# Row maxima on one core: loads of three rows in two places for two rows in three, and a table of places for the last 28 rows

## The chip, the core and the metric

The kernel runs on one core of one Trainium2 chip. The engines that matter: the sixteen DMA engines of the core, which bring data from HBM into the on-chip memory (SBUF, 128 partitions); SyncE (SP), which issues loads and the last store; ScalarE (ACT), which issues the other store; and VectorE (DVE), which reduces. GpSimd (POOL) only clears semaphores at the end, and TensorE has no work.

The metric is the time of one execution on the device, in microseconds (us), as the median of several runs.

## The reference

```
def reference(x):                      # x: 8192 x 8192, float32, normal
    return np.linalg.norm(x, ord=np.inf, axis=1)
```

The infinity norm of each row: the largest absolute value among its 8192 elements. 268.44 MB go in, 32 KB come out.

## The kernel before

Each of the 128 partitions holds 64 whole rows of `x` in the course of the run, 8192 elements (32 KB) each. VectorE's `reduce_max` with absolute values (L253) takes a stretch of a partition's data and leaves one number, or one per row when it gets several whole rows in one instruction. All data pass through one tile, `ring` (49664 elements per partition), and all results collect in `r_bulk` and `r_tail`.

**The bulk (L261 to L269).** 40 rows per partition come in 20 loads of `B` = 2 rows (16384 elements per partition, 8.4 MB). They go to `SLOTS` = 3 places of the ring in turn. Each load is followed by one reduction of two rows into `r_bulk`. A place is used again when its reduction is done, so two loads can be under way or queued while a third is being reduced.

**The end (`TAIL`, L20 to L31, and L272 to L317).** The last 24 rows per partition lie side by side as 196608 elements and come in 37 loads, listed in `TAIL` as (start in the data, width), the widths falling from 16384 to 512. A load need not hold whole rows: L272 to L280 cut each load into pieces at the row borders. A piece that isn't the last of its row is reduced to one number, which is written into the ring just ahead of the place where the row's last piece will land (`slot`); the row's last piece is then reduced together with those numbers into `r_tail`. The places are worked out in order around the ring (L283 to L294), each aligned to `PAD` = 128.

**Order.** SP issues all loads in the program's order. A load waits for the reductions that read the part of the ring that it overwrites (a semaphore that VectorE counts up), and, as there are eight semaphores for transfers, for the landing of the load eight before it. VectorE takes the reductions in program order and waits for each load's semaphore. `r_bulk` is stored from ACT after the reductions of the third last load (L314 to L317), `r_tail` from SP after the last one (L318).

Four functions that run over the finished program (L319 to L322) are the same in both kernels: they drop waits that another wait implies, move the first load ahead of the program's opening, let POOL do the ending, and leave VectorE out of the opening.

Of the kernel before, what the change touches and what calls it, by code (L numbers as in the profile page):

```python
# [16 lines left out]

HEAD, STEP = 32, 8

TAIL = [  # L20
    (0, 16384), (16384, 16384), (32768, 16384), (49152, 15488),
    (64640, 14336), (78976, 12800), (91776, 11392), (103168, 10112),
    (113280, 9088), (122368, 8064), (130432, 7296), (137728, 6528),
    (144256, 5760), (150016, 5248), (155264, 4608), (159872, 4096),
    (163968, 3712), (167680, 3328), (171008, 2944), (173952, 2688),
    (176640, 2432), (179072, 2176), (188416, 1920), (181248, 1792),
    (190336, 1536), (183040, 1408), (191872, 1280), (184448, 1152),
    (193152, 1024), (185600, 896), (194176, 768), (186496, 768),
    (194944, 640), (187264, 640), (195584, 512), (187904, 512),
    (196096, 512),  # L30
]  # L31


# [177 lines left out]
@with_exitstack  # L211
def kernel(
    ctx: ExitStack,
    tc: tile.TileContext,
    x: bass.AP,
    out: bass.AP,
    G: int = 4,
    B: int = 2,
    SLOTS: int = 3,
    PAD: int = 128,  # L220
):
    nc = tc.nc
    P = nc.NUM_PARTITIONS
    rows, cols = x.shape
    W = B * cols
    R = SLOTS * W + PAD * 4


    n_tail = sum(w for _, w in TAIL) // cols
    met = 0  # L230
    for lo, w in sorted(TAIL):
        assert lo == met
        met += w
    assert met == n_tail * cols
    n_bulk_rows = rows // P - n_tail
    assert n_bulk_rows % (G * B) == 0
    A = n_bulk_rows // (G * B)
    split = n_bulk_rows * P
    x_b = x[:split].rearrange("(a p n b) c -> a n p (b c)", p=P, a=A, n=G, b=B)
    out_b = out[:split].rearrange("(a p n b) -> p a (n b)", p=P, a=A, n=G, b=B)  # L240
    x_t = x[split:].rearrange("(p t) c -> p (t c)", p=P)
    out_t = out[split:].rearrange("(p t) -> p t", p=P)

    pool = ctx.enter_context(tc.tile_pool(name="sbuf", bufs=1))
    r_bulk = pool.tile([P, A, G * B], F32)
    r_tail = pool.tile([P, n_tail], F32)
    used = [HEAD, A * G * B, n_tail]
    gap = -sum(-(-n // STEP) * STEP for n in used) % PAD
    pool.tile([P, gap], F32, name="gap")
    ring = pool.tile([P, R], F32)  # L250

    def absmax(o, i):
        return nc.vector.reduce_max(  # L253
            out=o, in_=i, axis=X, apply_absolute_value=True
        )

    def after(ins, first, kind):
        info = mybir.DependencyInfo(kind, mybir.DependencyReason.SCHED_ONLY)
        tc.add_manual_dep(ins.ins, first.ins.name, info, reason="order")

    for a in range(A):  # L261
        for n in range(G):
            at = (a * G + n) % SLOTS * W
            t = ring[:, at : at + W]
            nc.sync.dma_start(out=t, in_=x_b[a, n])
            absmax(
                r_bulk[:, a, n * B : (n + 1) * B],
                t.rearrange("p (b c) -> p b c", b=B),
            )  # L269


    pieces = []  # L272
    for j, (at, w) in enumerate(TAIL):
        end = at + w
        while at < end:
            r = at // cols
            to = min(end, (r + 1) * cols)
            pieces.append((j, r, to - at))
            at = to
    of_row = [[k for k, s in enumerate(pieces) if s[1] == r] for r in range(n_tail)]  # L280


    here = A * G % SLOTS * W  # L283
    start, slot = [], []
    for j, (_, w) in enumerate(TAIL):
        first = next(s for s in pieces if s[0] == j)
        ks = of_row[first[1]]
        n_part = len(ks) - 1 if pieces[ks[-1]][0] == j else 0
        at = -(-(here + n_part) // PAD) * PAD
        if at + w > R:  # L290
            at = -(-n_part // PAD) * PAD
        start.append(at)
        slot.append(at - n_part)
        here = at + w  # L294

    for j, (src, w) in enumerate(TAIL):
        at = start[j]
        nc.sync.dma_start(out=ring[:, at : at + w], in_=x_t[:, src : src + w])
        here = [k for k, s in enumerate(pieces) if s[0] == j]
        offs = [at + sum(pieces[i][2] for i in here[:m]) for m in range(len(here))]  # L300
        todo = list(zip(here, offs))
        if slot[j] != at:

            todo = todo[1:] + todo[:1]
        for k, lo in todo:
            _, r, n = pieces[k]
            ks = of_row[r]
            if k == ks[-1]:
                frm = slot[j] if len(ks) > 1 else lo
                done = absmax(r_tail[:, r : r + 1], ring[:, frm : lo + n])  # L310
            else:
                to = slot[pieces[ks[-1]][0]] + ks.index(k)
                done = absmax(ring[:, to : to + 1], ring[:, lo : lo + n])
        if j == len(TAIL) - 3:  # L314

            ins = nc.scalar.dma_start(out=out_b, in_=r_bulk[:])
            after(ins, done, mybir.DependencyClass.Sync)  # L317
    nc.sync.dma_start(out=out_t, in_=r_tail[:])  # L318
    nc.at_finalize(drop_implied_waits)  # L319
    nc.at_finalize(start_first_load_early)  # L320
    nc.at_finalize(finish_on_pool)
    nc.at_finalize(open_without_vector)  # L322
# [30 lines left out]
```

## Time and profile before

| what | value |
|---|---|
| time, median of 3 runs | 626.67 us (626.62 to 627.07) |
| the profiled execution's own time | 626.65 us |
| its span, first to last instruction | 624.0 us |
| VectorE busy | 553.1 us, 76 instructions |
| 20 reductions of two rows | 344.4 us, 17220 ns each |
| loads | 57, 268.44 MB, 430 GB/s over the span |
| VectorE's waits for loads | 62.1 us before the bulk's reductions, 7.9 us later |

How to read it: "busy" is the time in which an engine executes; for the DMA queues it is the time that their packets took, as a share of sixteen engines' span. A packet is what one DMA engine moves for one descriptor. In the timeline the columns are start, duration, engine, line, operation, what it writes and reads with partitions x elements, how many were merged, and the idle time before them with what ended it. In the chain of waits they are start, duration, and what the chain went through. In the waits they are the engine and line, what it waited for, the total in us, how many times, and the longest. In the groups of instructions, the busy time in us, the mean duration in ns, and the idle time before them. "SPq" and "ACTq" are the queues from which SP and ACT issue transfers. The packed trace also has a record of each DMA packet (start, duration, size) and of each count that a transfer's engines add to its semaphore; sixteen such counts make a landing.

### The profile page before, as it was taken

Reading aid. Unit: us, or ns where it says so; the run is one execution under the profiler, and the core shown is the slowest. Engines: PE = TensorE matmul, PEld = TensorE weight load, DVE = VectorE, ACT = ScalarE, POOL = GpSimd, SP = SyncE. Lnnn points to the kernel's source line nnn. Section 1 sums busy time; section 2 is a strip of 40 time slices with the busy share of each in tenths; the row PEclk is TensorE's granted clock in tenths of the full one; section 3 lists DMA queues with packets and bytes.
Section 4 is the critical chain, followed back from the end, with each engine's and each line's share of the span. In section 5 each row is a group of like instructions: output and inputs, shape, how many; then the busy total and the mean of one; then the engine's idle time right before and its main releaser. Section 6 shows DMA issues by size and latency. Waiting matters only on the chain.

```text
span 624.0 us, 166 instructions
## 1 busy us (share of the span) xinstructions
DVE 553.1 (89%) x76; POOL 0.2 (0%) x4
## 2 busy tenths in 40 slices
DVE  0588988889988899888898888988899999999999
POOL 0000000000000000000000000000000000000000
DMA  9999999999999999999999999999999999999998
GB/s 403 454 420 454 420 441 433 408 466 403 471 403 454 420 454 420 450 424 429 445 408 466 403 466 408 454 420 454 409 435 445 422 436 428 429 427 431 429 425 343
DMA packets 8865, 268.47 MB, mean 430 GB/s; under 512 B 1568, under 2 KB 1568, under 8 KB 3488
## 3 DMA queue, kind: packets, MB, share of 16 engines
q1 hardware_dynamic: 8208, 268.44, 99.7%
q10 hardware_dynamic: 656, 0.02, 0.1%
q14 instruction: 1, 0.01, 0.0%
HBM read 268.44 MB, written 0.03 MB: 430 GB/s over the span
## 4 chain that ended last, share of the span: by engine, by line
DMA 61%; DVE 38%; issue 0%; DVEq 0%
DMA ring<-in_x_dram 61%; DVE r_bulk L253 19%; DVE ring L253 10%; DVE r_tail L253 9%; DVEq L348 0%
## 5 line engine op out<-in xcount | busy, mean ns | idle before, releaser
L253 DVE TENSOR_REDUCE r_bulk<-ring 128x2 f32<-128x16384 f32 x20 | 344.4, 17220 | 62.1 <-DMA ring<-in_x_dram 62.1
L253 DVE TENSOR_REDUCE r_tail<-ring 128x1 f32<-128x8192 f32 (+14 forms) x24 | 109.7, 4587 | 7.7 <-DMA ring<-in_x_dram 7.7
L253 DVE TENSOR_REDUCE ring<-ring 128x1 f32<-128x5248 f32 (+26 forms) x32 | 101.5, 3215 | 0.2 <-DMA ring<-in_x_dram 0.2
L337 POOL MEMSET const-bfloat16-1.0<- 128x1 bf16 x1 | 0.1, 101 | 0.0
L337 POOL MEMSET const-uint8-127<- 128x1 uint8 x1 | 0.1, 101 | 0.0
L337 POOL MEMSET const-float32-0.0<- 128x1 f32 x1 | 0.1, 98 | 0.2 <-issue 0.2
L337 POOL MEMSET const-float32-1.0<- 128x1 f32 x1 | 0.1, 98 | 0.0
## 6 DMA issues: line engine op xcount, KB each, us to landing
ring<-in_x_dram SPq DMA_DIRECT2D x1, 7744.0 KB, 39.6
ring<-in_x_dram SPq DMA_DIRECT2D x1, 7168.0 KB, 37.2
ring<-in_x_dram SPq DMA_DIRECT2D x1, 6400.0 KB, 33.0
ring<-in_x_dram SPq DMA_DIRECT2D x1, 5696.0 KB, 36.7
ring<-in_x_dram SPq DMA_DIRECT2D x1, 5056.0 KB, 41.0
ring<-in_x_dram SPq DMA_DIRECT2D x1, 4544.0 KB, 36.0
ring<-in_x_dram SPq DMA_DIRECT2D x1, 4032.0 KB, 31.9
ring<-in_x_dram SPq DMA_DIRECT2D x1, 3648.0 KB, 40.2
```

The source lines that it names most:

```text
L253: return nc.vector.reduce_max(out=o, in_=i, axis=X, apply_absolute_value=True)
L337: nc = _bacc.Bacc("TRN2", target_bir_lowering=False, num_devices=1)
```

## The change

Four edits, all in the tile kernel and its table:

- The bulk's loads are three rows wide (`B` = 3, 24576 elements per partition, 12.6 MB) and use two places (`SLOTS` = 2). There are 12 of them, for 36 rows.
- The end has 28 rows in 35 loads. `TAIL` now lists (place in the ring, start in the data, width); the places are no longer worked out. The widths fall from 24576 to 768. The ring has a fixed size, `R` = 52992.
- Where a load of the end holds several whole rows in a run, one reduction takes them together. With the wider loads of the bulk, VectorE has 50 reductions instead of 76.
- Each load is ordered behind the one before it (no semaphore), and a load whose row has numbers waiting ahead of its place is ordered behind the reduction that wrote them.

In the built program a load wider than 16384 elements per partition has two descriptors for each partition instead of one (128 x 2 x 12288 for a load of 24576).

```diff
 TAIL = [
-    (0, 16384), (16384, 16384), (32768, 16384), (49152, 15488),
-    (64640, 14336), (78976, 12800), (91776, 11392), (103168, 10112),
...
-    (194944, 640), (187264, 640), (195584, 512), (187904, 512),
-    (196096, 512),
+    (0, 0, 24576), (24576, 24576, 23552), (0, 49152, 20864),
+    (20864, 73728, 16384), (0, 90112, 16384), (37248, 106496, 11392),
+    (16384, 122880, 8192), (24576, 131072, 8192), (0, 139264, 8192),
+    (8192, 147456, 8192), (32768, 155648, 8192), (16384, 163840, 8192),
+    (24576, 172032, 7424), (0, 180224, 7040), (7040, 188416, 6016),
...
+    (51968, 48128, 1024), (38016, 228352, 1024), (43904, 203904, 896),
+    (50944, 72832, 896), (48512, 179456, 768),
 ]
...
-    B: int = 2,
-    SLOTS: int = 3,
+    B: int = 3,
+    SLOTS: int = 2,
+    R: int = 52992,
     PAD: int = 128,
...
-    R = SLOTS * W + PAD * 4
...
-    for a in range(A):
-        for n in range(G):
-            at = (a * G + n) % SLOTS * W
-            t = ring[:, at : at + W]
-            nc.sync.dma_start(out=t, in_=x_b[a, n])
-            absmax(
-                r_bulk[:, a, n * B : (n + 1) * B],
-                t.rearrange("p (b c) -> p b c", b=B),
-            )
+    loads = []
+
+    def load(lo, n, src):
+        ins = nc.sync.dma_start(out=ring[:, lo : lo + n], in_=src)
+        if loads:
+            after(ins, loads[-1], mybir.DependencyClass.NoSync)
+        loads.append(ins)
+
+    for k in range(A * G):
+        at = k % SLOTS * W
+        load(at, W, x_b[k // G, k % G])
+        absmax(
+            r_bulk[:, k // G, k % G * B : (k % G + 1) * B],
+            ring[:, at : at + W].rearrange("p (b c) -> p b c", b=B),
+        )
...
             r = at // cols
-            to = min(end, (r + 1) * cols)
-            pieces.append((j, r, to - at))
-            at = to
+            n = min(end, (r + 1) * cols) - at
+            if n == cols:
+                n = (end - at) // cols * cols
+            pieces.append((j, r, n))
+            at += n
...
+    part = {}
+    for j, (at, src, w) in enumerate(TAIL):
+        load(at, w, x_t[:, src : src + w])
+        if slot[j] != at:
+            after(loads[-1], part[slot[j]], mybir.DependencyClass.Sync)
...
-            if k == ks[-1]:
-                frm = slot[j] if len(ks) > 1 else lo
-                done = absmax(r_tail[:, r : r + 1], ring[:, frm : lo + n])
-            else:
+            if k != ks[-1]:
                 to = slot[pieces[ks[-1]][0]] + ks.index(k)
                 done = absmax(ring[:, to : to + 1], ring[:, lo : lo + n])
+                part[slot[pieces[ks[-1]][0]]] = done
+            elif len(ks) > 1:
+                done = absmax(r_tail[:, r : r + 1], ring[:, slot[j] : lo + n])
+            else:
+                b = n // cols
+                t = ring[:, lo : lo + n].rearrange("p (b c) -> p b c", b=b)
+                done = absmax(r_tail[:, r : r + b], t)
```

## The prediction, made before the changed kernel had run

> **What bounds the kernel now.** I read the page first: the busy lines and the queues.
>
> ```profile
> span 624.0 us, 166 instructions
> ## 1 busy us (share of the span) xinstructions
> DVE 553.1 (89%) x76; POOL 0.2 (0%) x4
> ...
> q1 hardware_dynamic: 8208, 268.44, 99.7%
> ...
> q14 instruction: 1, 0.01, 0.0%
> ```
>
> The load queue q1 keeps its sixteen DMA engines busy for 99.7% of the span; VectorE (DVE) is busy for 89%. The bytes are fixed, so a gain must come from the first 2 us, the last 2 us, or small costs between packets. The waits say who is early and who is late, then the timeline gives the rhythm.
>
> ```profile
> DVE r_bulk L253 <- DMA ring<-in_x_dram: 62.1, 20, 22.1
> ```
>
> ```profile
> 22.11 17.22 DVE L253 TENSOR_REDUCE r_bulk<-ring 128x2 f32<-128x16384 f32 x1 [22.11 <-DMA ring<-in_x_dram]
> 41.40 17.22 DVE L253 TENSOR_REDUCE r_bulk<-ring 128x2 f32<-128x16384 f32 x1 [2.08 <-DMA ring<-in_x_dram]
> 60.74 17.22 DVE L253 TENSOR_REDUCE r_bulk<-ring 128x2 f32<-128x16384 f32 x1 [2.12 <-DMA ring<-in_x_dram]
> ...
> 572.92 10.08 DVE L253 TENSOR_REDUCE ring<-ring 128x1 f32<-128x5248 f32 x2 [0.24 <-DMA ring<-in_x_dram]
> ...
> 621.95 1.28 DVE L253 TENSOR_REDUCE r_tail<-ring 128x1 f32<-128x519 f32 x2
> 622.07 0.41 ACTq L316 DMA_DIRECT2D out_dram<-r_bulk  x1
> 623.26 0.35 SPq L318 DMA_DIRECT2D out_dram<-r_tail  x1
> ```
>
> VectorE waits about 2.1 us for every load of two rows. The landings behind those starts, 22.08 to 447.19 us over 22 intervals, are 19.32 us apart. The chain of waits shows how early a load is issued:
>
> ```profile
> 39.34 0.02 issue
> 39.35 40.76 DMA ring<-in_x_dram
> 80.11 0.02 issue
> ```
>
> A load issued at 39.35 lands at 80.11, behind the load that lands at 60.72: SP issues 21.4 us before the queue would run dry. So DMA is the bound with a large reserve, and the end is the last landing (622.41 in the trace) plus 0.82 us of VectorE (to 623.23) plus 0.77 us to the end of the span.
>
> **The change part by part.** Sums are against the profiled span, 624.0; that execution took 626.65, and the median is 626.67, so I add 2.67 to a span.
>
> *Descriptors and loads.* In the packet records each load is cut into one packet per partition and one 4-byte semaphore packet per engine: 57 x 144 = 8208, the page's count. A packet of 65536 B starts 2.416 us after the one before it on its engine, one of 2048 B 0.080 us: 36.8 ps per byte plus 0.0047 us per packet; the semaphore packet adds 0.006. The built program turns every load wider than 16384 into two packets per partition: 15 such loads, 47 in all. An engine then handles 15 x 16 + 32 x 8 = 496 data packets for 456, so 40 x 0.0047 = +0.19, and ten semaphores fewer, 10 x 0.006 = -0.06. Bounds: -0.44 if a load costs 0.044 whatever its packets (8 x 0.0047 + 0.006), +0.19 if the semaphores are free.
>
> *The instruction fetch.* The one q14 packet after the start comes at 570.05 and takes 0.31 us on one DMA engine. Until then the first and last engine of a load finish 0.85 to 0.98 us apart; at the landing of 572.89 it is 1.29, and that landing comes 0.34 us later than its bytes ask (6.56 us against 5248/16384 x 19.32 + 0.03 = 6.22). VectorE's 0.24 us wait at 572.92 shows it: the fetch fell on the slowest engine. It comes 0.85 us after VectorE began its 48th reduction, with no other engine's instruction near. The new program has 50 reductions and reaches the 48th after the loads have been read, so I take -0.33; 0 if the fetch is another engine's or comes earlier.
>
> The Trainium skill ("Runtime: NRT & Kernel Launch", section "Instruction fetch mechanics") says that instruction memory is refilled in blocks of 256 instructions, mostly hidden. The trace differs: 8 KB, with 76 VectorE instructions, and not hidden. By the page no instruction count here would need a fetch, this term would be 0 and the time 627.0.
>
> *The end.* The rows:
>
> ```profile
> L253 DVE TENSOR_REDUCE ring<-ring 128x1 f32<-128x768 f32 x2 | 1.8, 942 | 0.0
> ...
> L253 DVE TENSOR_REDUCE r_tail<-ring 128x1 f32<-128x519 f32 x2 | 1.3, 683 | 0.0
> ```
>
> The last load is 768 wide instead of 512. It lands 768/16384 x 19.28 + 0.044 = 0.95 us after the one of 896, whose reduction holds VectorE 0.99 us (1.075 less 0.083 that neighbours overlap). So the last one starts some 0.07 us after landing and takes 0.943: 1.01 to 1.04 instead of 0.82, +0.20. The two stores wait for the same things as before. 26 VectorE instructions fewer save 26 x 0.06 us (a back-to-back step is 1.0417 ns per element plus 0.06) = 1.6 us, worth nothing: VectorE waits for landings at both ends.
>
> *Two places instead of three.* This removes the reserve. Per load of three rows the transfer is 1.5 x 19.32 + 0.04 = 29.0 us; the reduction 17.22 plus one more row (17.22 - 8.69 = 8.53) = 25.75, and 0.05 for two semaphores. SP can issue load k only when load k-2 is reduced: 29.0 - 25.8 = 3.2 us before load k-1 lands, not 21.4. This holds at twelve handoffs: loads 3 to 12 of the bulk and the table's first two. Two others are tighter. The table's third load (20864 at place 0) waits for the reduction of the first while the second, only 23552 wide (27.8 us), flies: 27.8 - 25.8 = 2.0. Its fifth (16384 at place 0) waits for two rows of the third, 17.2 + 0.1, against 19.3 for the fourth: 2.0 again. All others have 7 us or more. SP has nothing else queued behind these waits than later loads, whose places come free later still.
>
> What a handoff costs depends on the time from SP's issue until a DMA engine runs at full rate. The slowest engine ends its last packet 0.34 us before a landing, so it has 2.9 us at the twelve and 1.7 at the two; the fastest has 0.9 less, but it may also idle 0.9 without moving the end. The trace shows no load that comes to a nearly empty queue in mid-stream. Lower end: the final stores, issued at 622.07 and 623.26, have their first packets 0.96 and 0.84 us later. Upper end: the very first load, issued at 0.00, has first packets at 0.99 to 2.22, and by its landings (21.17 to 22.08, less 0.32 and 8 x 2.416) reaches full rate 1.5 to 2.4 us after issue. I take 1.0: at a handoff the queue is running and the reads of the last packets cover the start, as in the stores; the first load also had to start sixteen idle engines (its first packets took 2.5 to 3.2 us, later ones 2.42). At 1.0 the slowest engine never empties; a fast one idles 0.2 us, or some 0.8 with a fresh start, inside its 0.9. Cost 0; by the upper end 2 x (2.4 - 1.7) = 1.4 to 1.5.
>
> **Sum:** 624.0 + 0.19 - 0.06 - 0.33 + 0.20 + 0 = 624.0, so 626.7: no change. Own range 626.2 to 627.3.
>
> **The rivals.**
>
> *A: the two tight handoffs run dry.* For it: the nearest HBM load, the first, needed 2.4 us on its slowest engine, over the 1.7 at hand. Against it: half of that is a cold start. Price from 1.0 at 2.2 us to 1.5 at 2.4: 627.7 to 628.2. It decides from 1.7 us on.
>
> The Trainium skill ("DMA: Bandwidth & Descriptors", section "Latency and other measured facts") puts the first byte of a hardware queue at about 0.6 us and an HBM access under high load at 2 us. No run here shows either in mid-stream. Together 2.6 us, an estimate: 0.9 at each tight handoff and 628.5.
>
> *B: every handoff runs dry.* One mechanism, slower than before: under a saturated HBM a fresh load needs over 2.9 us. The twelve handoffs pay the excess each, the two tight ones 1.2 more each. At 3.2: 12 x 0.3 less what the engines' spread absorbs, some 2 to 4 us, and 2 x 1.5 = 5 to 7: about 632. Against it: no row above 2.4.
>
> *C: loads are priced per load, not per packet.* -0.44 instead of +0.13: 626.1. Against it: the two-point fit above.
>
> **How the numbers follow.** Forecast 0.42, A 0.28, B 0.20, C 0.06, something faster that I don't see 0.04. Changes under 0.2% (1.25 us; about what a measurement of this kernel can tell from no change) are 625.4 to 627.9. Same: the forecast, C, and 0.10 of A below 627.9: 0.58. Slower: 0.18 of A and B: 0.38. Faster: 0.04, since the whole start and end offer hardly 1.2 us. The range reaches from C's 626.1, less 0.2, over all of A and the start of B: 625.9 to 630.0, leaving out some 0.18.
>
> **What would show it.** Handoffs right: VectorE waits 3.2 us before each bulk reduction but the first, landings 29.0 us apart, and 27.8 and 24.6 for the table's second and third load. A shows as 25.3 instead of 24.6 (third load) and 20.0 instead of 19.3 (fifth); B as bulk intervals above 29.1 and a q1 share below 99.5%. The fetch term is right if no q14 packet comes before 620 us. The end is right if the last reduction ends 1.0 us after the last landing. The prediction is wrong if any handoff opens a gap on the slowest engine.

## The result, and the profile after

| | before | after |
|---|---|---|
| time, median of 6 runs each | 626.72 us (626.62 to 627.13) | 637.91 us (637.30 to 639.51) |
| ratio, 95% interval | | 1.0181 (1.0168 to 1.0195) |
| span of the profiled execution | 624.0 us | 635.2 us |
| last landing | 622.41 us | 633.44 us |

The change costs 11.2 us, 1.8%. The forecast was no change, and the time lies outside the range. The page of the changed kernel, span, busy lines and queues:

```profile
span 635.2 us, 126 instructions
...
DVE 551.0 (87%) x50; POOL 0.2 (0%) x4
...
q1 hardware_dynamic: 8688, 268.44, 99.0%
q10 hardware_dynamic: 400, 0.02, 0.0%
```

VectorE does as much as before. The load queue's share falls from 99.7% to 99.0%: the DMA engines now have gaps. Gaps are the smaller part of the loss: 99.0% of 635.2 is 628.8 us of packet time per engine, against 622.1 before, so packets also take some 6.7 us longer in all. There is no q14 line any more. The waits put most of VectorE's idle time before the bulk, as before, but with the wait before the first load 31.8 instead of 22.1 us:

```profile
DVE r_bulk L256 <- DMA ring<-in_x_dram: 74.2, 12, 31.8
```

The timeline of the changed kernel, VectorE's reductions in the bulk and at the start of the table:

```profile
31.79 25.75 DVE L256 TENSOR_REDUCE r_bulk<-ring 128x3 f32<-128x24576 f32 x1 [31.79 <-DMA ring<-in_x_dram]
60.79 25.75 DVE L256 TENSOR_REDUCE r_bulk<-ring 128x3 f32<-128x24576 f32 x1 [3.24 <-DMA ring<-in_x_dram]
90.11 25.75 DVE L256 TENSOR_REDUCE r_bulk<-ring 128x3 f32<-128x24576 f32 x1 [3.57 <-DMA ring<-in_x_dram]
...
178.32 25.75 DVE L256 TENSOR_REDUCE r_bulk<-ring 128x3 f32<-128x24576 f32 x1 [3.29 <-DMA ring<-in_x_dram]
208.82 25.75 DVE L256 TENSOR_REDUCE r_bulk<-ring 128x3 f32<-128x24576 f32 x1 [4.75 <-DMA ring<-in_x_dram]
...
388.44 25.75 DVE L256 TENSOR_REDUCE r_tail<-ring 128x3 f32<-128x24576 f32 x1 [5.18 <-DMA ring<-in_x_dram]
416.33 17.22 DVE L256 TENSOR_REDUCE r_tail<-ring 128x2 f32<-128x16384 f32 x1 [2.13 <-DMA ring<-in_x_dram]
```

A wait of 3.2 us means that the load came on the 29.0 us beat. Waits of 4.8 and 5.2 mean that it landed 1.5 and 2.0 us late: 178.32 to 208.82 is 30.5 us. Thirteen loads on a beat of 28.98 us (1.5 times the 19.32 of before) would have the last one in at 31.77 + 12 x 28.98 = 379.5; it lands at 388.42, so 8.9 us go here. By the 29.00 us that lead_7 (below) keeps it is 8.6. The chain of waits of the changed kernel (start, duration, what it went through) shows the new limit:

```profile
57.57 32.51 DMA ring<-in_x_dram
90.08 0.02 issue
90.11 25.77 DVE r_bulk L256
...
175.05 33.75 DMA ring<-in_x_dram
208.80 0.02 issue
208.82 25.77 DVE r_bulk L256
...
354.06 34.36 DMA ring<-in_x_dram
...
414.22 27.34 DMA ring<-in_x_dram
...
458.83 23.18 DMA ring<-in_x_dram
```

Load and reduction alternate: a load is issued when a reduction has freed its place, and the next reduction waits for that load. The load issued at 175.05 takes 33.75 us, although its bytes need 29.0 and the load ahead of it lands after 3.24. From here on, the *lead* is the time from a load's issue to the landing of the load ahead, and the *loss* is what its landing is late against the beat.

Of the 11.03 us by which the last landing moved, the eleven handoffs up to 388.42 hold 8.9, the table's second load 0.1, its third (issued at 414.22, lands 25.26 us after the one ahead, its bytes ask 24.64) 0.6, and its fifth (issued at 458.83, 21.10 for 19.32) 1.8. With +0.13 for packets and -0.33 for the fetch as predicted that is 11.2, 0.2 more than measured: the price of the bulk's added packets (29.00 instead of 28.98 us per load) is in the 8.9 already and is counted twice.

### The profile page after: what moved, and what is told of

It is laid out like the page before. It is cut to its first block, busy times and chain, and to the rows that moved or that the text cites. A ratio compares the mean times of both kernels' runs of the same rounds, so it can differ in the third digit from the quotient of the medians.

```text
span 635.2 us, 126 instructions
## 1 busy us (share of the span) xinstructions
DVE 551.0 (87%) x50; POOL 0.2 (0%) x4
## 4 chain that ended last, share of the span: by engine, by line
DMA 50%; DVE 50%; DVEq 0%; issue 0%
DMA ring<-in_x_dram 50%; DVE r_bulk L256 24%; DVE r_tail L256 17%; DVE ring L256 8%; DVEq L361 0%
## 5 line engine op out<-in xcount | busy, mean ns | idle before, releaser
L256 DVE TENSOR_REDUCE r_bulk<-ring 128x3 f32<-128x24576 f32 x12 | 309.0, 25753 | 74.2 <-DMA ring<-in_x_dram 74.2
L256 DVE TENSOR_REDUCE r_tail<-ring 128x1 f32<-128x8192 f32 (+11 forms) x22 | 170.2, 7783 | 9.2 <-DMA ring<-in_x_dram 9.2
L256 DVE TENSOR_REDUCE ring<-ring 128x1 f32<-128x7168 f32 (+15 forms) x16 | 72.6, 4578 | 0.1
```

What stands on the lines that cost most here:

```text
L256: return nc.vector.reduce_max(out=o, in_=i, axis=X, apply_absolute_value=True)
```

## The experiments

Medians are set against the kernel before, run on the same chip (626.6 to 626.7 in each batch).

| kernel | leads in the bulk, us | loss in the bulk, us | time, us | ratio, 95% interval |
|---|---|---|---|---|
| after | 3.2 to 5.1 | 8.9 | 637.91 | 1.0181 (1.0168 to 1.0195) |
| one_row_loads | 3.1 to 6.5 | 9.5 | 639.32 | 1.0194 (1.0177 to 1.0211) |
| lead_3_7 | 3.7 to 5.1 | 6.2 | 636.11 | 1.0157 (1.0137 to 1.0177) |
| lead_4 | 4.2 to 4.4 | 0.55 | 630.60 | 1.0061 (1.0048 to 1.0075) |
| lead_5 | 5.2 | 0.25 | 630.29 | 1.0057 (1.0041 to 1.0072) |
| lead_7 | 7.3 | 0.28 | 630.64 | 1.0059 (1.0044 to 1.0075) |
| half_bulk_reduce | 16.0 | 0.44 | 630.29 | 1.0059 (1.0044 to 1.0074) |
| released_by_parts | 21 and 32 | 0.52 | 628.53 | 1.0030 (1.0019 to 1.0041) |
| all_leads_long | 21 and 32 | 0.55 | 627.28 | 1.0011 (1.0002 to 1.0019) |
| before_two_places | 2.0 to 6.0 | 22.5 | 650.31 | 1.0375 (1.0359 to 1.0390) |
| two_places_lead_4 | 4.2 to 4.5 | 0.26 | 626.92 | 1.0005 (0.9996 to 1.0014) |
| before_two_descriptors | 21 | 0.7 | 627.62 | 1.0016 (1.0007 to 1.0026) |
| two_queues | no load ahead | | 671.76 | 1.0718 (1.0701 to 1.0734) |

Leads and losses are those of the one profiled execution. The loss is against 28.98 us per load, 19.32 us for loads of two rows. In the kernels whose leads are all 5 us or more, what is listed is not loss at handoffs but mostly the price of added packets, 0.02 to 0.04 us per load; released_by_parts and all_leads_long also have one landing each that is about 0.25 us late with a lead of 21 us.

**half_bulk_reduce: the same loads, a long lead.** From the changed kernel:

```diff
-            ring[:, at : at + W].rearrange("p (b c) -> p b c", b=B),
+            ring[:, at : at + W].rearrange("p (b c) -> p b c", b=B)[:, :, : cols // 2],
```

> The changed kernel, but each bulk reduction reads only the first half of each of its three rows (the other half of 36 rows per partition is left out of the result). Loads, places and descriptors are those of the changed kernel; a reduction takes about 12.9 us instead of 25.75, so a bulk load is issued about 16 us before the one ahead of it lands, instead of 3.2. Theory 1 (too little lead: a load issued 3 us ahead reaches the DMA engines too late): the 8.9 us that the bulk lost vanish, the table's third and fifth load still lose about 2.4; 629 us. Theory 2 (the 272 descriptors of a load take too long to be written, but only when the lead is short): the same, 629. Theory 3 (loads of two descriptors per partition, or the new row pitch, are slower by themselves): still about 638.

Its timeline, the bulk's second and third reduction:

```profile
60.60 12.95 DVE L256 TENSOR_REDUCE r_bulk<-ring 128x3 f32<-128x12288 f32 x1 [16.06 <-DMA ring<-in_x_dram]
89.60 12.95 DVE L256 TENSOR_REDUCE r_bulk<-ring 128x3 f32<-128x12288 f32 x1 [16.05 <-DMA ring<-in_x_dram]
```

Every wait is 16 us and the beat is 29.0. Loads, descriptors and places are those of the changed kernel, so nothing in the loads alone makes the loss; Theory 3 falls. The table's two tight handoffs, which the edit leaves alone, still lose 3.9 us (25.52 for the third load, 22.31 for the fifth), which is the 3.9 us of the span above before's.

**one_row_loads: no wide descriptors, the same lead.** From the changed kernel, each bulk load as three:

```diff
-        load(at, W, x_b[k // G, k % G])
+        for i in range(B):
+            load(at + i * cols, cols, x_b[k // G, k % G, :, i * cols : (i + 1) * cols])
```

> The changed kernel, but each bulk load is issued as three loads of one row with one descriptor per partition, all three still released by the one reduction of three rows. The lead of the first of them stays 3.2 us. Theory 1 (lead alone): 637 to 638, as the changed kernel. Theory 2 (the late engines are late because a load's 272 descriptors are written one after another): the first load's 144 descriptors arrive in half the time, most of the bulk's 8.9 us vanish; 629 to 631.

Its timeline, the bulk's second to fourth reduction:

```profile
60.56 25.75 DVE L256 TENSOR_REDUCE r_bulk<-ring 128x3 f32<-128x24576 f32 x1 [3.27 <-DMA ring<-in_x_dram]
90.79 25.75 DVE L256 TENSOR_REDUCE r_bulk<-ring 128x3 f32<-128x24576 f32 x1 [4.47 <-DMA ring<-in_x_dram]
119.94 25.75 DVE L256 TENSOR_REDUCE r_bulk<-ring 128x3 f32<-128x24576 f32 x1 [3.40 <-DMA ring<-in_x_dram]
```

The same late landings (60.56 to 90.79 is 30.2 us) with the same short waits. How a load is cut into descriptors doesn't matter here; Theory 2 falls. The time is 1.3 us over what was expected; 1.05 us of its loss fall on a load that was issued 24 us ahead, and the lead doesn't explain these.

**before_two_places: the kernel before, with the third place taken away and nothing else.**

```diff
-    SLOTS: int = 3,
+    SLOTS: int = 2,
...
-    R = SLOTS * W + PAD * 4
+    R = 3 * W + PAD * 4
```

> The kernel before with two places instead of three for the bulk's loads of two rows (one descriptor per partition). A load is issued 19.3 - 17.3 = 2.0 us before the one ahead lands. Theory 1 (lead alone): each of some 18 handoffs loses at least what the changed kernel's two handoffs with 2.0 us lost (0.7 and 1.75): 640 to 658 us. Theory 2 (number of descriptors): 144 descriptors come in time; 627 to 631.

Its timeline and its load queue on the page:

```profile
41.33 17.22 DVE L253 TENSOR_REDUCE r_bulk<-ring 128x2 f32<-128x16384 f32 x1 [2.06 <-DMA ring<-in_x_dram]
63.09 17.22 DVE L253 TENSOR_REDUCE r_bulk<-ring 128x2 f32<-128x16384 f32 x1 [4.54 <-DMA ring<-in_x_dram]
82.59 17.22 DVE L253 TENSOR_REDUCE r_bulk<-ring 128x2 f32<-128x16384 f32 x1 [2.28 <-DMA ring<-in_x_dram]
104.96 17.22 DVE L253 TENSOR_REDUCE r_bulk<-ring 128x2 f32<-128x16384 f32 x1 [5.15 <-DMA ring<-in_x_dram]
```

```profile
q1 hardware_dynamic: 8208, 268.44, 97.7%
```

Two places alone cost 23.7 us. The lead is 2.0 here and 3.2 in the changed kernel, whose wider loads soften the loss: a reduction of three rows leaves more of its transfer over than one of two. Single losses at leads between 2 and 3 us run from nothing to 3.94.

**before_two_descriptors: the price of packets by itself.** The kernel before, with each bulk load in two descriptors of 32 KB per partition:

```diff
-    x_b = x[:split].rearrange("(a p n b) c -> a n p (b c)", p=P, a=A, n=G, b=B)
+    x_b = x[:split].rearrange("(a p b n) c -> a n p b c", p=P, a=A, n=G, b=B)
...
-            nc.sync.dma_start(out=t, in_=x_b[a, n])
+            nc.sync.dma_start(
+                out=t.rearrange("p (b c) -> p b c", b=B), in_=x_b[a, n]
+            )
```

> The kernel before, three places, but each bulk load takes rows that are not neighbours, so that it has two descriptors of 32 KB per partition, 272 in all, as in the changed kernel, with the lead of 21 us kept. Theories 1 and 2: only the price per descriptor, 20 x 8 x 0.0047 = 0.75 us; 627.4. Theory 3 (two descriptors are slow by themselves): 632 or more.

The span is 624.8, 0.8 above before's (1.0 in the medians). 20 x 8 = 160 more packets per engine at the prediction's 0.0047 are 0.75: the term holds, with a lead of 21 us and no loss beside it.

**lead_4, lead_5, lead_7: where the loss begins.** The changed kernel, with the bulk's reductions a little shorter, so that each load is issued earlier; lead_4:

```diff
-            ring[:, at : at + W].rearrange("p (b c) -> p b c", b=B),
+            ring[:, at : at + W].rearrange("p (b c) -> p b c", b=B)[:, :, 320:],
```

and with 640 and 1312 in the place of 320 in lead_5 and lead_7.

> The changed kernel, but each bulk reduction leaves out the first 320 elements of each of its three rows, so that it takes 1.0 us less and a bulk load is issued about 4.2 us before the one ahead of it lands, instead of 3.2. The table's tight handoffs are unchanged (half_bulk_reduce: 630.3 with a lead of 16 us in the bulk). Theory 1a (a load needs some 4 to 5 us from issue until its slowest DMA engine runs at full rate, and the loss at a handoff is what is missing of that): the bulk still loses some 0.3 to 0.5 us at each of ten handoffs; 632 to 635. Theory 1b (there is no threshold; each engine needs many packets queued, so that the loss falls off slowly with the lead): 636 to 637.

> As lead_4 with 640 elements of each row left out: a lead of about 5.2 us. Theory 1a: the bulk's loss is nearly gone; 630 to 631.5. Theory 1b: 634 to 636.

> As lead_4 with 1312 elements of each row left out: a lead of about 7.3 us. Theory 1a: nothing is lost in the bulk, as in half_bulk_reduce; 629.5 to 631. Theory 1b: 632 to 634.

The timeline of lead_4:

```profile
60.43 24.75 DVE L256 TENSOR_REDUCE r_bulk<-ring 128x3 f32<-128x23616 f32 x1 [4.23 <-DMA ring<-in_x_dram]
89.47 24.75 DVE L256 TENSOR_REDUCE r_bulk<-ring 128x3 f32<-128x23616 f32 x1 [4.29 <-DMA ring<-in_x_dram]
118.69 24.75 DVE L256 TENSOR_REDUCE r_bulk<-ring 128x3 f32<-128x23616 f32 x1 [4.47 <-DMA ring<-in_x_dram]
```

One microsecond less of VectorE per load ends the loss in the bulk: the beat is 29.0 again and the chain's loads take 4.2 + 29.0 = 33.2. All three kernels have the same time, and what they still lose is at the table's tight handoffs. For lead_4 the expectation under the higher limit missed: the limit lies lower than the theory put it.

**lead_3_7: between.** As lead_4, with 160 in the place of 320.

> As lead_4 (630.6 us; no loss left in the bulk) with 160 elements of each row left out: a lead of about 3.7 us. The changed kernel has 3.2 and loses 8.9 us in the bulk. If the limit is the latest engine's descriptors, seen up to 3.4 us after the issue, an engine that ends its load 0.34 + 0.5 us before the landing still runs dry now and then: 630.5 to 634. A smooth dependence on the lead would give 634.

Its timeline:

```profile
60.53 25.25 DVE L256 TENSOR_REDUCE r_bulk<-ring 128x3 f32<-128x24096 f32 x1 [3.70 <-DMA ring<-in_x_dram]
90.52 25.25 DVE L256 TENSOR_REDUCE r_bulk<-ring 128x3 f32<-128x24096 f32 x1 [4.73 <-DMA ring<-in_x_dram]
119.52 25.25 DVE L256 TENSOR_REDUCE r_bulk<-ring 128x3 f32<-128x24096 f32 x1 [3.75 <-DMA ring<-in_x_dram]
```

This missed too: half a microsecond of lead brings back 2.7 of the 8.9 us, not most of it. A lead of 3.7 still loses 1.0 us here (60.53 to 90.52 is 30.0 us), and 1.0 to 1.4 us at four other handoffs of the bulk with leads of 3.7 to 3.9. The next half microsecond, to a lead of 4.2, brings back 5.6: the loss falls off steeply there.

**two_places_lead_4: the same limit with other loads.** before_two_places, its bulk reductions cut by `[:, :, 1056:]`.

> before_two_places (650.3 us with a lead of 2.0 us), but each bulk reduction leaves out the first 1056 elements of each of its two rows, so that the lead is about 4.2 us. Theory 1a (what counts is a fixed time from issue, over by 4.2 us): the loss vanishes here too, with one descriptor per partition; 626.5 to 628. Rival (the time needed grows as the share of a load, or falls with the descriptors: the changed kernel's limit is its own): 630 or more, or no loss already below 4.

626.92 us, no longer told from before. Two places, 20 loads of one descriptor per partition and a lead of 4.2 lose 0.26 us in 20 handoffs, where a lead of 2.0 lost 22.5. So it is the lead, whatever the size and cut of the loads. It is not the lead alone: in before_two_places a load with a lead of 4.9 us, behind one whose engines ended 3.3 us apart, still lost 0.8 us.

**released_by_parts: the change, with its places freed earlier.** The changed kernel, complete, with each bulk load and its reduction in two parts (two rows, one row), and the table's first and third load cut likewise:

```diff
-    (0, 0, 24576), (24576, 24576, 23552), (0, 49152, 20864),
+    (0, 0, 16384), (16384, 16384, 8192), (24576, 24576, 23552),
+    (0, 49152, 16384), (16384, 65536, 4480),
...
-        load(at, W, x_b[k // G, k % G])
-        absmax(
...
-        )
+        for lo, hi in ((0, 2), (2, 3)):
+            b0, b1 = at + lo * cols, at + hi * cols
+            load(b0, b1 - b0, x_b[k // G, k % G, :, lo * cols : hi * cols])
+            absmax(
+                r_bulk[:, k // G, k % G * B + lo : k % G * B + hi],
+                ring[:, b0:b1].rearrange("p (b c) -> p b c", b=hi - lo),
+            )
```

> The changed kernel with its two places of three rows, but each bulk load is made as a load of two rows and a load of one row, each reduced by an instruction of its own, so that the first two rows of a place are free 8.6 us before the third; the table's first load is cut in the same way and its third at 16384. The shortest lead is then about 7 us, in the bulk over 20. VectorE has 63 reductions. Theory 1 (lead alone): no handoff loses anything; 626.7 plus 0.3 for packets and the last reduction, 626.5 to 627.3. Rival (the two places or the row pitch of the new layout cost something by themselves): 629 or more.

The same ring and the same data with 9.4 us less, and 1.2 us more than expected. One lead was misjudged: VectorE was busy with the load of 23552 until 432.2, so the 16384 at place 0 was still issued 2.0 us before the landing ahead. The chain of waits of this kernel names it:

```profile
449.45 22.85 DMA ring<-in_x_dram
```

It takes 22.85 for 2.0 + 19.3 us: 1.5 us lost at the one tight handoff that was left.

**all_leads_long: that one mended too.** The two 16384-wide loads to place 0 (one is the cut third) are cut into pairs of 8192:

```diff
-    (0, 49152, 16384), (16384, 65536, 4480),
-    (20864, 73728, 16384), (0, 90112, 16384), (37248, 106496, 11392),
+    (0, 49152, 8192), (8192, 57344, 8192), (16384, 65536, 4480),
+    (20864, 73728, 16384), (0, 90112, 8192), (8192, 98304, 8192), (37248, 106496, 11392),
```

> released_by_parts had one tight handoff left: its load of 16384 at place 0, issued 2.0 us before the one ahead of it landed, took 20.84 us to land instead of 19.3, and the time was 1.9 us over the kernel before. Here that load and the one whose reduction releases it are each cut into two loads of one row. The shortest lead is 7 us. VectorE has 65 reductions. Theory 1 (lead alone): 626.7 plus about 0.3 for packets and the last reduction, 626.6 to 627.2, not to be told from the kernel before. Rival (the new layout costs something by itself): over 628.

The queues on its page:

```profile
q1 hardware_dynamic: 9200, 268.44, 99.7%
q10 hardware_dynamic: 400, 0.02, 0.0%
q14 instruction: 1, 0.01, 0.0%
```

The loss at the handoffs is gone and the share is 99.7% again. The time is 0.1 us over the expected range and can be told from the kernel before (0.11% slower, interval 0.02 to 0.19%). What is left is, as far as the trace shows, packets, the longer last reduction, and the instruction fetch, which is back: at 583.17, and the load that lands then comes 0.7 us late (0.3 before) with the engines' spread up from 0.38 to 1.03. No kernel that ran beats the one before.

**two_queues: a try at why the start is late.** The changed kernel, every second bulk load issued from ACT:

```diff
-        ins = nc.sync.dma_start(out=ring[:, lo : lo + n], in_=src)
+        eng = nc.scalar if n == W and len(loads) % 2 else nc.sync
+        ins = eng.dma_start(out=ring[:, lo : lo + n], in_=src)
```

> The changed kernel, but every second bulk load is issued from ACT instead of SP, so that a load and the one ahead of it stand in different queues on the same sixteen DMA engines. The lead stays 3.2 us. If the late engines are late because a load's descriptors queue behind those of the load ahead in the same queue: the bulk's loss falls; 629 to 632. If the time goes in getting a load started on engines that carry full traffic, whichever queue it is in: 636 to 639.

Its timeline, the first four bulk reductions, two merged in each line:

```profile
58.88 51.41 DVE L256 TENSOR_REDUCE r_bulk<-ring 128x3 f32<-128x24576 f32 x2 [58.88 <-DMA ring<-in_x_dram]
119.90 51.41 DVE L256 TENSOR_REDUCE r_bulk<-ring 128x3 f32<-128x24576 f32 x2 [9.61 <-DMA ring<-in_x_dram]
```

Inconclusive for its question: neither of the expected ranges came. The engines take packets of the two queues in turn (in the packet records from 5 to 55 us every one of 448 packets is followed on its engine by one of the other queue), so the first two loads share the bandwidth and land almost together, at 58.86 and 60.61 us, instead of at 31.8 and 60.8; with both places filled at once nothing is left to load while VectorE reduces. It shows only that two places rely on one queue working in order.

## Why the prediction was wrong

**The step that failed** is "Two places instead of three", and in it the time a handoff needs. The leads were right: 3.2 us where the load ahead is on time, 2.1 measured at both tight handoffs, where 2.0 was worked out. The price was wrong: "I take 1.0" from issue to full rate, with "Upper end ... 1.5 to 2.4 us", so that "the slowest engine never empties". I named the final stores (0.84 and 0.96) and the first load (2.4 at most) as the nearest rows, and reasoned that a running queue starts faster than an idle one. The runs show a start that can be much slower. In the packet records around the load issued at 175.05, engines that had run dry get their first packets 2.22 to 3.43 us after issue, and those take 2.27 to 3.04 us where a packet in mid-stream takes 1.815. The latest one alone explains the landing: issue 175.05 + 3.43 + 2.83 for its first packet + 15 x 1.812 for the others + 0.34 to the landing = 208.83; measured 208.80. So from issue to full rate it is 3.43 + (2.83 - 1.815) = 4.4 us, nearly twice the upper end. It is no constant: in before_two_places the load that lost 3.94 us had a first packet 4.14 us after issue that took 4.21 us instead of 2.42, 5.9 us in all. Neither of the two nearest rows had the traffic of a running load beside it, and the bound should have been left open upwards.

The Trainium skill ("DMA: Bandwidth & Descriptors", section "Latency and other measured facts") has 0.6 us to a first byte and 2 us for an HBM access under high load; the 2.6 us estimated from these is nearer than my 1.0 and still too short: measured at the handoff of 175.05 are 3.43 to the latest first packet and 4.4 to full rate. It would have asked for 628.5, and 637.91 came.

**Rival B was the mechanism, at too small a price.** Its signs came: bulk intervals up to 30.9 us instead of 29.0, and a q1 share of 99.0%. It was priced at 3.2 us to full rate and less "what the engines' spread absorbs". At the handoff of 175.05 the spread absorbs nothing: the slowest engine ends its old work 2.95 us after the issue, and 4.4 less 2.95 is the 1.5 us by which the load was late. An engine that is early runs dry first, and if its new packet comes late it is the last one of the next load. The spread at a landing grew from 0.57 us at the second load to 3.07 at the thirteenth, so the fastest engine ends its old work 2.28 us after issue at the first handoff and 0.85 at the eleventh, at leads of 3.2 and 3.4 us. The losses at short leads grow with it, from 0.3 to 2.0 us.

**Why 8.9 and not eleven times 2.** A load that lands 1.5 us late leaves the next issue a lead of 4.7 (30.5 - 25.8), and with that almost nothing is lost (0.25 us at most); then the lead is 3.2 again. In the timeline, waits of 3.3 and 4.8 alternate. Five handoffs hold 7.9 of the 8.9 us.

**Rival A** was right for the table's third load (25.3 said, 25.26 measured) and short at its fifth (20.0 said, 21.10 measured). The match at the third is luck: both had a lead of 2.1 us, and in lead_4 the third took 26.99.

**What held.** The packets: 0.8 us for 160 per engine against 0.75. The fetch: no q14 packet in the changed kernel. The end: the last landing is at 633.44 and the last reduction ends at 634.48, 1.04 us, where 1.01 to 1.04 was worked out. The beat of 29.0 where a lead was long, and 27.8 for the table's second load (27.88). Only one term of the sum was wrong, and it was the one that had been put at 0.

**What is open.** Why an engine that runs dry under traffic gets its next packet 1 us after issue in one case (the earliest in before_two_places) and 3.4 in another. The run with two queues didn't tell. Nor does a run show why packets that follow such a start take longer, which is the larger part of the 11 us.

## What to carry to other kernels

Where DMA is the bound, ask for each load how long before the landing of the load ahead it is issued. In these runs 4.2 us cost next to nothing where the engines kept within 1 us of each other, and 3.7 us cost about a microsecond at every second handoff, so fewer but wider buffers are safe only if the consumer frees them that early; freeing a wide buffer in two parts did it without more memory. Price a start under load by a row that has the load beside it, and if there is none, leave the bound open.

## What the runs showed of the hardware that was not expected

- The loss sets in steeply. It is best told by the fastest engine: in the bulk of lead_4 and two_places_lead_4 it had work until 3.41 to 3.65 and 3.06 to 3.26 us after the issue, and no handoff lost more than 0.26 us; landings 0.25 us late also occur with leads of 21 us. Where it had work until 2.85 us or less, losses ran from 0 to 3.94 us.
- The engines, 0.57 and 0.59 us apart at the changed kernel's first two landings, drift to 3.07 us apart through late starts. The tight handoff to the table's third load brings them back to 0.65, the one to its fifth sets them 1.65 apart, and from there on, with long leads, the spread stays: it is still 1.6 us at 620 us.
- The instruction fetch follows VectorE's count. It comes during the 47th or 48th reduction: at 570.04 us before, 592.43 in before_two_places, 593.86 with 63 reductions, 583.17 with 65. The load that lands then came 0.3 us late before and 0.7 us late in all_leads_long. The Trainium skill ("Runtime: NRT & Kernel Launch", section "Instruction fetch mechanics") has blocks of 256 instructions, mostly hidden; here it comes far earlier, and is not hidden in a kernel that DMA bounds.
